# Low weight parts of every second unit: a VectorE subtraction replaced by a ScalarE copy and an accumulating DMA

## The chip, the cores and the metric

The kernel runs on one core of one Trainium2 chip. The time is device microseconds of one launch, from the first to the last instruction of the core and what lies around it; lower is better. The core has TensorE (matrix products, PE in the profile), VectorE (DVE), ScalarE (ACT), GpSimd (POOL) and SyncE (SP), each with a queue of its own that it works through in order, and 16 DMA engines that all queues share.

## What is computed

One block of a streaming encoder over 256 frames of width 2048, in float32. In the reference's words, cut to what matters:

```python
x = x + 0.5 * swiglu(rms_norm(x, ffn1_norm), ffn1_w_gate, ffn1_w_up, ffn1_w_down)
proj = rms_norm(x, mix_norm) @ w_in
x = x + concatenate([pool_mixer(...), gla_mixer(...)]) @ w_out
x = x + mem_cross_attention(rms_norm(x, xattn_norm), rms_norm(mem, mem_norm), w_q, w_kv, w_o)
x = x + 0.5 * swiglu(rms_norm(x, ffn2_norm), ffn2_w_gate, ffn2_w_up, ffn2_w_down)
return rms_norm(x, final_norm)
```

The feed-forward width is 5632, there are 256 memory tokens, 4 heads. What takes the time are the products with the large weights; all weights together are some 400 MB, and each is read once.

## The kernel before

**Two parts for each number.** TensorE's fast float32 form, fp32r, keeps fewer bits of a number than float32. So every operand is written as a sum of two fp32r tiles: the high part (the number rounded by the write) and the low part (number minus high part). A product is the sum of three: high x high, high x low and low x high. Activations are stored as such pairs in `xs` and `ys`, weights are split while they stream in.

**Groups and units.** Weights stream in groups of 512 rows by 512 columns (1 MB), loaded by SP into one of three `raw` buffers (`wload`, L317). A group has two units of 256 rows each (part 0 and part 1). For each unit `split_unit` (L971) makes a high tile `wh` and a low tile `wl` of 128 x 1024: through `split` (L217), ScalarE casts raw to `wh` (L218), and VectorE subtracts, `wl = raw - wh` (L219). There are four buffers of each (`AHEAD` + 1), so the tiles of a unit can only be written when TensorE has done with those of the unit four back.

**Two kinds of block.** In `block_a` (L259) the weights are the stationary operand: a unit is eight pairs of matmuls, one of `wh` with 512 columns (high and low activations side by side), one of `wl` with 256 columns. In `block_b` (L290) the activations are stationary, and a unit is twelve matmuls of 512 columns, one in three with `wl`. A block has mostly four groups (K = 2048) and ends with an eviction from PSUM by ScalarE and VectorE (`joined`, L252, and what follows it; the residual additions at L398).

**What sets the order.** `Stream.emit` (L69) runs through the units in order. Before the matmuls of unit u it emits the splits up to unit u+3, and behind the split of a group's last part the load of the group three further on. The load therefore waits for the last reader of the `raw` buffer that it overwrites. Evictions and norms are put between units by counts. The program is then scheduled as a whole with a timeline model (L1011), which may place instructions of one engine in another order than they are written, where the dependences allow it.

Of the kernel before, what the change touches and what calls it, by code (L numbers as in the profile page):

```python
# [9 lines left out]
AF = mybir.ActivationFunctionType  # L10
ALU = mybir.AluOpType
# [73 lines left out]
def build(ctx, tc, I, out):  # L85
    nc = tc.nc
# [130 lines left out]
    def split(hi, lo, src):  # L217
        nc.scalar.copy(hi, src)  # L218
        nc.vector.tensor_tensor(out=lo, in0=src, in1=f32(hi), op=ALU.subtract)  # L219
# [751 lines left out]
    def split_unit(g, part, last, own):  # L971
        raw = raws.pop(g) if last else raws[g]
        hi, lo = (
            wpool.tile([P, 2, NB], F32R, tag=t, name=f"{t}{g}_{part}", bufs=st.AHEAD + 1)
            for t in ("wh", "wl")
        )
        if own:
            own((hi, lo), raw)
        else:
            step = 1 if g == part == 0 else 2  # L980
            for k in range(0, 2, step):
                src = raw[:, 2 * part + k : 2 * part + k + step, :]
                split(hi[:, k : k + step, :], lo[:, k : k + step, :], src)
        return hi, lo
# [4 lines left out]
    for g in range(st.RAW):  # L989
        load(g)  # L990
    st.emit(load, split_unit)


# [30 lines left out]
```

## Time and profile before

| | us |
|---|---|
| time before, median of 2 runs (2193.71 to 2194.71) | 2194.21 |
| the profiled execution's own time | 2194.78 |
| its span, first to last instruction | 2192.7 |
| TensorE busy | 2173.8 |
| VectorE busy | 1320.3 |
| ScalarE busy | 1037.2 |
| GpSimd busy | 14.3 |

The granted TensorE clock is 0.998 over the span. The profile is of one execution. A line such as `L218 ACT CAST wh<-raw ... x756 | 792.5, 1049 | 1015.2 <-PE pa L280 746.6` is a group of instructions: line 218, on ScalarE, writes a `wh` tile from a `raw` tile, 756 times, 792.5 us busy in sum, 1049 ns each; ahead of them ScalarE sat idle for 1015.2 us, and 746.6 of it ended when TensorE's matmuls of L280 released it. The chain of waits is followed back from the last instruction and says on which engine the time of the end hangs. In the list of DMA issues the last number is the time from issue to landing. In a timeline a row has its start, its length, and in brackets how long its engine idled before and what released it.

### The profile page before, as it was taken

Reading aid. Unit: us, or ns where it says so; the run is one execution under the profiler, and the core shown is the slowest. Engines: PE = TensorE matmul, PEld = TensorE weight load, DVE = VectorE, ACT = ScalarE, POOL = GpSimd, SP = SyncE. Lnnn points to the kernel's source line nnn. Section 1 sums busy time; section 2 is a strip of 40 time slices with the busy share of each in tenths; the row PEclk is TensorE's granted clock in tenths of the full one; section 3 lists DMA queues with packets and bytes.
Section 4 is the critical chain, followed back from the end, with each engine's and each line's share of the span. In section 5 each row is a group of like instructions: output and inputs, shape, how many; then the busy total and the mean of one; then the engine's idle time right before and its main releaser. Section 6 shows DMA issues by size and latency. Waiting matters only on the chain.

```text
span 2192.7 us, 29165 instructions
## 1 busy us (share of the span) xinstructions
PE 2173.8 (99%) x11990; PEld 1876.5 (86%) x11990; DVE 1320.3 (60%) x1518; ACT 1037.2 (47%) x1273; POOL 14.3 (1%) x43
## 2 busy tenths in 40 slices
PE   8999999999999999999999999999999999999997
PEld 7888888888888888888888888888888888888886
DVE  6656556565566777667665555655655565545655
ACT  6444344443444546465455444554443444434443
POOL 0000000000000000000000000000000000000001
PEclk9999999999999999999999999999999999999999
DMA  7555555555555555565555445555555555555553
GB/s 252 185 184 188 192 184 182 191 181 188 189 191 176 191 175 176 157 221 179 189 175 177 168 160 186 191 176 185 182 189 193 191 189 182 187 194 189 192 185 122
DMA packets 205901, 404.79 MB, mean 185 GB/s; under 512 B 8644, under 2 KB 11816, under 8 KB 205384
## 3 DMA queue, kind: packets, MB, share of 16 engines
q1 hardware_dynamic: 205736, 402.92, 55.1%
q8 instruction: 94, 1.54, 0.3%
q14 instruction: 39, 0.32, 0.0%
q10 hardware_dynamic: 32, 0.01, 0.0%
HBM read 400.80 MB, written 2.10 MB: 184 GB/s over the span
## 4 chain that ended last, share of the span: by engine, by line
PE 98%; DMA 1%; DVE 1%; ACT 0%; SPq 0%; issue 0%; DVEq 0%; ACTq 0%
PE pa L280 79%; PE pb L306 14%; PE pe L880 3%; DMA raw<-in_ffn_w_gate 1%; PE pv L816 1%; PE pl L781 1%; DMA rows<-in_x 0%; PE ps L207 0%; PE pa L539 0%; DVE wl L219 0%; PE po L662 0%; PE pb L850 0%; PE tm L740 0%; PE pq L649 0%; DVE Xn L929 0%; PE pn L199 0%
## 5 line engine op out<-in xcount | busy, mean ns | idle before, releaser
L219 DVE TENSOR_TENSOR wl<-raw,wh 128x1024 fp32r<-128x1024 f32 (+1 forms) x755 | 922.1, 1222 | 789.4 <-ACT wh L218 785.2
L280 PE MATMUL pa<-xs,wh 128*128 128x512 f32 x3712 | 1309.6, 398 | 2.1 <-DVE xs L211 2.0
L218 ACT CAST wh<-raw 128x1024 fp32r<-128x1024 f32 (+1 forms) x756 | 792.5, 1049 | 1015.2 <-PE pa L280 746.6
L280 PE MATMUL pa<-xs,wl 128*128 128x256 f32 x3712 | 1031.4, 281 | 0.0
L280 PEld LDWEIGHTS pa<-xs,wh 128*128 128x128 f32 x3712 | 694.2, 188 | 166.0 <-DVE xs L211 3.1
L280 PEld LDWEIGHTS pa<-xs,wl 128*128 128x128 f32 x3712 | 701.5, 189 | 5.9
L280 PE MATMUL pa<-ys,wh 128*128 128x512 f32 x1216 | 428.6, 398 | 0.0
L280 PE MATMUL pa<-ys,wl 128*128 128x256 f32 x1216 | 338.2, 281 | 0.0
L280 PEld LDWEIGHTS pa<-ys,wh 128*128 128x128 f32 x1216 | 227.5, 188 | 54.7
L280 PEld LDWEIGHTS pa<-ys,wl 128*128 128x128 f32 x1216 | 229.7, 189 | 1.8
L306 PE MATMUL pb<-wh,ys 128*128 128x512 f32 x512 | 157.9, 389 | 0.0
L306 PE MATMUL pb<-wh,xs 128*128 128x512 f32 x384 | 122.5, 393 | 0.4 <-DVE ys L211 0.4
L306 PEld LDWEIGHTS pb<-wh,ys 128*128 128x128 f32 x512 | 96.1, 188 | 19.9
L254 ACT COPY c<-pa 128x512 f32<-128x512 f32 x116 | 67.7, 584 | 67.4 <-PE pa L280 67.4
L306 PE MATMUL pb<-wl,ys 128*128 128x512 f32 x256 | 99.6, 389 | 0.0
L306 PEld LDWEIGHTS pb<-wh,xs 128*128 128x128 f32 x384 | 71.9, 188 | 15.3 <-DVE ys L211 0.6
L306 PE MATMUL pb<-wl,xs 128*128 128x512 f32 x192 | 75.0, 390 | 0.0
L880 PE MATMUL pe<-wh,ys 128*128 128x512 f32 x192 | 59.3, 389 | 0.0
L306 PEld LDWEIGHTS pb<-wl,ys 128*128 128x128 f32 x256 | 48.1, 188 | 10.0
L255 DVE TENSOR_TENSOR t<-pa,c 128x512 f32<-128x512 f32 x64 | 44.0, 688 | 18.3 <-ACT c L254 18.3
L398 DVE SCALAR_TENSOR_TENSOR X<-pa,X 128x512 f32<-128x512 f32 x80 | 51.5, 686 | 0.1
L880 PEld LDWEIGHTS pe<-wh,ys 128*128 128x128 f32 x192 | 36.0, 188 | 7.5
(174 smaller groups left out, 810.4 us busy)
## 6 DMA issues: line engine op xcount, KB each, us to landing
raw<-in_ffn_w_up SPq DMA_DIRECT2D x88, 1024.0 KB, 5.0
raw<-in_ffn_w_gate SPq DMA_DIRECT2D x86, 1024.0 KB, 4.9
raw<-in_ffn_w_down SPq DMA_DIRECT2D x84, 1024.0 KB, 4.9
raw<-in_w_in SPq DMA_DIRECT2D x32, 1024.0 KB, 5.3
raw<-in_xattn_w_kv SPq DMA_DIRECT2D x32, 1024.0 KB, 5.2
raw<-in_w_out SPq DMA_DIRECT2D x16, 1024.0 KB, 4.9
raw<-in_xattn_w_q SPq DMA_DIRECT2D x16, 1024.0 KB, 4.9
raw<-in_xattn_w_o SPq DMA_DIRECT2D x16, 1024.0 KB, 4.9
```

Of the source, the lines that this page charges most:

```text
L218: nc.scalar.copy(hi, src)
L219: nc.vector.tensor_tensor(out=lo, in0=src, in1=f32(hi), op=ALU.subtract)
L254: nc.scalar.copy(c, ps[:, :, S:])
L255: nc.vector.tensor_tensor(out=dst, in0=ps[:, :, :S], in1=c, op=ALU.add)
L280: nc.tensor.matmul(o, w, x, start=k == 0 and i == 0, stop=last and i == 1)
L306: nc.tensor.matmul(held["ps"][:, h, :], a, w[:, kk, :], start=k == 0 and i == 0, stop=k == n_k - 1 and i == 2,)
L398: nc.vector.scalar_tensor_tensor(out=xk, in0=part, scalar=scale, in1=xk, op0=ALU.mult, op1=ALU.add)
L781: nc.tensor.matmul(ps[:, t, :M], ys[:, 4 * h + d, a, tok], xa["K"][:, d, b, :], start=i == 0, stop=i == 11,)
L816: nc.tensor.matmul(ps[:, d, :S], xa["V"][:, m, a, col], xa["PT"][:, m, b, :], start=i == 0, stop=i == 5,)
L880: nc.tensor.matmul(acc_ps[nb][:, h, :], a, w[:, kk, :], start=nb in first and kk == 0 and i == 0, stop=k == nk - 2 and kk == 1 and i == 2,)
```

## The change

Only `split_unit` changes. For part 1 of every group from group 8 on, except a group with a split of its own, the low part is made without VectorE. ScalarE casts raw to `wh` as before, then writes `wl` as -1 times raw, which the write rounds to the negative high part; then a DMA that GpSimd issues adds the raw weights to `wl`, from SBUF to SBUF. The sum is again raw minus its high part. Part 0 of every group, the first eight groups, and everything else stay as they are written.

```diff
@@ -976,6 +976,11 @@
         )
         if own:
             own((hi, lo), raw)
+        elif g >= 8 and part == 1:
+            src = raw[:, 2 * part : 2 * part + 2, :]
+            nc.scalar.copy(hi, src)
+            nc.scalar.activation(lo, src, AF.Copy, scale=-1.0)
+            nc.gpsimd.dma_start(out=lo, in_=src, accum_op=ALU.add)
         else:
             step = 1 if g == part == 0 else 2
             for k in range(0, 2, step):
```

## The prediction

> **What bounds the kernel now.** I read the page's busy times first, then the chain that ended last, then its groups.
>
> ```profile
> span 2192.7 us, 29165 instructions
> PE 2173.8 (99%) x11990; PEld 1876.5 (86%) x11990; DVE 1320.3 (60%) x1518; ACT 1037.2 (47%) x1273; POOL 14.3 (1%) x43
> ...
> PE 98%; DMA 1%; DVE 1%; ACT 0%; SPq 0%; issue 0%; DVEq 0%; ACTq 0%
> PE pa L280 79%; PE pb L306 14%; PE pe L880 3%; DMA raw<-in_ffn_w_gate 1%; PE pv L816 1%; PE pl L781 1%; DMA rows<-in_x 0%; PE ps L207 0%; PE pa L539 0%; DVE wl L219 0%; PE po L662 0%; PE pb L850 0%; PE tm L740 0%; PE pq L649 0%; DVE Xn L929 0%; PE pn L199 0%
> ...
> L219 DVE TENSOR_TENSOR wl<-raw,wh 128x1024 fp32r<-128x1024 f32 (+1 forms) x755 | 922.1, 1222 | 789.4 <-ACT wh L218 785.2
> ...
> L218 ACT CAST wh<-raw 128x1024 fp32r<-128x1024 f32 (+1 forms) x756 | 792.5, 1049 | 1015.2 <-PE pa L280 746.6
> ```
>
> TensorE is 98% of the chain; VectorE, the engine that is relieved, is 1% of it, some 22 us of the span. So the edit can gain at most those 22 us, and it loses whatever makes TensorE wait. VectorE's subtraction mostly waits for ScalarE's high part, and ScalarE's high part mostly waits for TensorE to give a buffer back: both engines run after TensorE, with time to spare. How much to spare is the question, and the timeline of one stretch answers it.
>
> ```profile
> 994.50 1.05 ACT L218 CAST wh<-raw 128x1024 fp32r<-128x1024 f32 x1 [0.44 <-PE pa L280]
> 997.39 1.05 ACT L218 CAST wh<-raw 128x1024 fp32r<-128x1024 f32 x1 [1.84 <-PE pa L280]
> ...
> 999.72 0.40 PE L280 MATMUL pa<-ys,wh 128*128 128x512 f32 x1
> 999.96 0.28 PE L280 MATMUL pa<-ys,wl 128*128 128x256 f32 x1
> ...
> 1000.08 0.40 PE L280 MATMUL pa<-ys,wh 128*128 128x512 f32 x1
> ...
> 1000.16 1.05 ACT L218 CAST wh<-raw 128x1024 fp32r<-128x1024 f32 x1 [1.71 <-PE pa L280]
> ...
> 1001.24 1.23 DVE L219 TENSOR_TENSOR wl<-raw,wh 128x1024 fp32r<-128x1024 f32 x1 [0.70 <-ACT wh L218]
> ...
> 1002.98 1.05 ACT L218 CAST wh<-raw 128x1024 fp32r<-128x1024 f32 x1 [1.77 <-PE pa L280]
> ...
> 1005.82 1.05 ACT L218 CAST wh<-raw 128x1024 fp32r<-128x1024 f32 x1 [1.78 <-PE pa L280]
> ```
>
> One pair of matmuls (high, then low) takes 0.36 us (999.72 to 1000.08), a unit of eight pairs 2.83 us; the casts follow each other at 2.82 and 2.84 us. There are four wh and four wl buffers, so a cast starts when TensorE has ended the unit four back, and its own unit begins three units later: 3 x 2.83 = 8.5 us. Cast and subtraction take 1.05 + 1.23 of it. About 6 us are spare at every unit, for both parts.
>
> **The change part by part.** It applies to one unit in two from group 8 on: by the code 369 units.
>
> *VectorE loses* 369 x 1.222 = 451 us of 1320. *ScalarE gains* a second pass over the same tile. The nearest rows are its other activations:
>
> ```profile
> L210 ACT ACTIVATE xs<-X,gains 128x256 fp32r<-128x256 f32 x64 | 28.9, 498 | 3.1 <-DVE X L398 3.0
> L229 ACT ACTIVATE t<-X 128x512 f32<-128x512 f32 x21 | 13.0, 617 | 0.0
> ```
>
> 256 further elements cost 0.12 to 0.21 us (617 - 498; CAST: (1049 - 617)/2), so 128x1024 takes 0.86 to 1.05 us; I take the cast's 1.05. ScalarE becomes 1037 + 387 = 1424 us, 65% of the span, hidden in the 1015 us that it idles before L218. If that cover went, each 0.1 us would come on top of the wait below.
>
> *The accumulating DMA* takes the subtraction's place between ScalarE and TensorE. No such DMA is in the trace, so it is bounded by the plain ones.
>
> ```profile
> q1 hardware_dynamic: 205736, 402.92, 55.1%
> ...
> raw<-in_w_out SPq DMA_DIRECT2D x16, 1024.0 KB, 4.9
> ...
> raw<-in_ffn_w_down SPq DMA_DIRECT2D x8, 512.0 KB, 4.3
> ...
> out<-Xn SPq DMA_DIRECT2D x8, 256.0 KB, 2.2
> ```
>
> A packet of about 2 KB takes 0.551 x 16 x 2192.7 / 205736 = 0.094 us of one DMA engine. A 1 MB load is 512 packets, 32 for each engine, 3.0 us; of its 4.9 us to landing 1.9 are not data. The accumulate writes 512 KB, and to add it must read raw and wl. If that costs as much as a copy: 16 x 0.094 = 1.5 us, with 1.9 landing after 3.4 us. If both reads pass one after the other: 3.0 us, landing after 4.9. The engines are in use by weight loads for 55% of the time; where the two meet and share, I give each half, so 3.0 becomes 3.0 / (1 - 0.55/2) = 4.1 us and the landing 1.9 + 4.1 = 6.0 us. Behind a whole load it would be 1.9 + 3.0 + 3.0 = 7.9 us. Ends: 3.4 and 7.9 us. I take 6.0, nearest to the 1 MB row, because it moves 1 MB in and 0.5 MB out, and because what no row shows (the add itself, GpSimd's issue) can only lengthen it.
>
> [...]
>
> *What is moved: TensorE's order.* The compiled order of the changed kernel is not that of before with one wait changed. In 118 of the 369 units TensorE's low-part matmuls now stand behind work of the next unit: the last half group of a block runs two high matmuls, then the next block's first unit, and only then its other 14. That widens the window of these units and narrows that of the unit which takes over their buffers. I count, unit by unit, the matmuls between the moment at which the negative copy may start (buffer given back, high part done) and the first matmul on the new low part, at 0.24 us for a 512-column and 0.12 for a 256-column matmul. In the commonest narrow place these are 14 leftover matmuls (2.36 us), one unit (2.83) and two high matmuls (0.47), less the high copy's 1.05: 4.6 us. All 369 windows: 42 average 4.6 us, 16 average 5.6, 10 average 6.4, 60 average 7.5, the other 241 are 8 us or more.
>
> The negative copy, the DMA and some 0.25 us of signalling must fit in: 1.05 + 6.0 + 0.25 = 7.3 us. The sum: 42 x (7.3 - 4.6) = 113; 16 x 1.7 = 27; 10 x 0.9 = 9; the rest fits. Together 149 us of TensorE waits, in some 70 places. All matmuls behind the waiting one wait too, and nothing makes it up, since the chain is TensorE.
>
> *Covered moves.* SP's load of group g+3 waited for the subtraction and now waits for the accumulate's landing, 1.05 + 6.0 - 1.2 = 5.8 us later:
>
> ```profile
> ACT wh L218 <- DMA raw<-in_ffn_w_gate: 7.3, 4, 3.6
> ```
>
> ```profile
> SPq L317 <- DVE wl L219: 1817.1, 348, 8.7
> ```
>
> These two rows are from the waits of the compute engines and of the DMA queue (total us, times, longest). ScalarE waited for a load 4 times in all; SP, on the other hand, always waited for its buffer. From a buffer's release to the cast that needs its next load are five units, 14.2 us, of which 0.1 + 1.05 + 1.23 + 4.9 = 7.3 are used; 6.9 spare against 5.8, and the cast itself has 6 us more ahead of TensorE. So it costs nothing; without that cover 1 us of lateness costs up to 1 us per group. GpSimd's queue holds nothing else in these stages than the next accumulates, each long after the last; its seven final-norm products come when the last accumulate is done. SP's queue keeps its order.
>
> The profiled execution took 2194.78 us, 2.1 more than its span and 0.6 above the median of 2194.21. Predicted: 2194.8 + 149 = 2344 us.
>
> **The rivals.**
>
> *The accumulate is hidden (not slower).* Place: the 42 windows of 4.6 us. If it lands 3.4 us after issue, as a copy would, 1.05 + 3.4 + 0.25 = 4.7 us and the loss is 42 x 0.1 = 4 us: 2198 us. For this speaks the 256 KB row's 2.2 us; against it the 512 KB row's 4.3. It decides at 4.3 us: then 42 x 1.0 + a little = 44 us, 2%. A gain beyond 2% would need 44 us from VectorE's 22, which I give 1 in 100.
>
> *The DMA engines become the bound.* Loads use 3.0 us of each engine per group; a group lasts two units, 5.66 us. With two reads the accumulate brings it to 6.0, which alone would be 369 x 0.34 = 125 us, still inside the forecast. If the adding costs twice that again (6.0 us), each of 369 groups takes 9.0 us, and the time is 2195 + 369 x 3.3 = 3400; at 4.5 us for the accumulate, 7.5 per group, 2870. For it speaks that one load fills the engines while it lasts:
>
> ```profile
> 1002.00:1004.25 2.25, 2.25 (x15) 1.92 (x14) 0.65 (x2) 1.05 (x1) 0.00 (x0) 1.00 0.98 333
> ```
>
> In this stretch of 2.25 us a load holds 98% of the engines at 333 GB/s, so an accumulate that falls there must push it aside. Against it: the engines idle for the other 45%, and three raw buffers let loads and accumulates take turns.
>
> *ScalarE becomes late.* Where blocks end, evictions queue between its casts, and a second pass of 1.05 us adds to each. With about 94 blocks (376 groups, most blocks of four) and one pass late at each, 94 x 1.05 = 99 us on top of the forecast: 2440. Against it: 1015 us idle before L218.
>
> **How the numbers follow.** Forecast (landing after 4.3 to 7.9 us) 0.62; hidden 0.22, of it 0.01 a gain over 2%; DMA engines as the bound 0.13; ScalarE late 0.03. About 2% is what a measurement of this kernel can tell from no change. So slower 0.62 + 0.13 + 0.03 = 0.78, same 0.21, faster 0.01. At 7.9 us the need is 9.2, and the classes give 42 x 4.6 + 16 x 3.6 + 10 x 2.8 + 60 x 1.7 + 143 x 1.1 (of the 241, those near 8.1) = 538 us, less what one stall gives to the next window in the same block, about a tenth: 484, so 2680, the high end. The low end is 2200, in the hidden case. Outside lie most of the DMA-bound case and the lowest part of the hidden one.
>
> **What would show it.** After: VectorE near 870 us and ScalarE near 1420; 369 new DMAs landing about 6 us after issue; TensorE's idle time before low-part matmuls of changed units near 150 us, on fewer than 100 places, put down to the DMA; DMA share near 0.8 to 0.95. Wrong would be: no TensorE idle time (hidden); waits at nearly every changed unit with the DMA share at its ceiling (the DMA engines); waits of TensorE put down to the high part (ScalarE).

## The result and the profile after

The changed kernel takes 2474.85 us (median of 2 runs, 2465.56 and 2484.13) against 2194.21: a ratio of 1.128, with a 95% interval of 1.110 to 1.146. Forecast were 2344 in a range of 2200 to 2680. The profiled execution is the longer one, 2484.13 us.

The page of the changed kernel first: busy times, DMA share by slices, DMA queues, and the chain that ended last.

```profile
span 2482.3 us, 30449 instructions
PE 2264.5 (91%) x11990; PEld 1920.2 (77%) x11990; DVE 885.2 (36%) x1149; ACT 1376.5 (55%) x1642; POOL 332.3 (13%) x412
...
DMA  7988999899898888899898999889899888898997
...
q1 hardware_dynamic: 205736, 402.92, 47.9%
q0 software_dynamic: 53136, 193.49, 41.1%
...
DMA 42%; PE 33%; issue 19%; ACT 5%; POOL 1%; DVE 1%; SPq 0%; POOLq 0%; ACTq 0%; DVEq 0%
DMA wl<-raw 37%; PE pa L280 23%; PE pb L306 7%; ACT wl L982 3%; DMA raw<-in_ffn_w_down 2%; PE pe L880 1%; POOL wl L983 1%; DMA raw<-in_ffn_w_up 1%; DMA raw<-in_w_out 1%; DMA raw<-in_w_in 1%; DMA raw<-in_ffn_w_gate 0%; ACT wh L981 0%; DMA rows<-in_x 0%; DMA raw<-in_xattn_w_o 0%; ACT wh L218 0%
```

VectorE and ScalarE moved by what the change takes and gives, and neither matters. The chain, which was TensorE to 98%, is now a transfer to 42%, and 37 of the 42 are the new one, `wl<-raw`. The span grew by 289.6 us. TensorE's busy time explains 90.7 of them (2264.5 - 2173.8), its idle time the other 198.9. The same page's groups (busy and mean ns, then idle before them with what ended it) and its DMA issues (KB each, median us from issue to landing) say where that idle time stands:

```profile
L280 PE MATMUL pa<-xs,wh 128*128 128x512 f32 x3712 | 1330.7, 405 | 0.5 <-DVE xs L211 0.5
L280 PE MATMUL pa<-xs,wl 128*128 128x256 f32 x3712 | 1025.2, 288 | 120.7 <-DMA wl<-raw 120.3
...
L982 ACT ACTIVATE wl<-raw 128x1024 fp32r<-128x1024 f32 x369 | 390.0, 1057 | 103.3 <-PE pb L306 74.9
...
L280 PE MATMUL pa<-ys,wl 128*128 128x256 f32 x1216 | 335.5, 289 | 50.8 <-DMA wl<-raw 50.3
...
L306 PE MATMUL pb<-wl,ys 128*128 128x512 f32 x256 | 103.3, 403 | 18.2 <-DMA wl<-raw 18.2
...
wl<-raw POOLq DMA_DIRECT2D x369, 512.0 KB, 6.1
raw<-in_ffn_w_up SPq DMA_DIRECT2D x88, 1024.0 KB, 5.7
```

TensorE stands still before low parts (`wl`) and hardly ever before high parts (0.5 us), and what it stands for is the landing of the accumulate. Matched one by one with the matmuls of the written kernel, there are 102 such waits of over half a microsecond, all on low parts that the change makes. Measured from the start of one matmul to the start of the next, less the 0.24 us that a matmul takes, they come to 214 us. The waits of the engines (total us, times, longest) name them again and show who else is held up:

```profile
PEld pa L280 <- DMA wl<-raw: 211.6, 104, 5.2
POOL wl L983 <- DMA wl<-raw: 209.5, 41, 7.6
...
ACT wh L218 <- DMA raw<-in_ffn_w_down: 73.9, 33, 4.7
ACT wh L218 <- DMA raw<-in_ffn_w_gate: 69.9, 39, 4.0
...
ACT wh L218 <- DMA raw<-in_ffn_w_up: 52.5, 29, 3.8
```

ScalarE's casts waited for loads 4 times in 7.3 us before; now these three rows alone have 101 waits and 196 us. The POOL row is no such wait, though it names one accumulate as waiting for another: in the trace all 41 of these issues start 0.29 to 0.31 us after ScalarE has written the negative copy, as nearly all the others do.

Most of the other 91 us, TensorE being busy for longer, comes from its clock. The mean granted clock is 0.968, against 0.998 before; 0.032 x 2482.3 - 0.002 x 2192.7 = 75 us. The rest is the difference between the two ways of measuring the waits (214 against 199 us). The timeline of TensorE at one wait, and the table of stretches behind it (length, then busy us of PE, PEld, DVE, ACT, POOL; granted clock; DMA share; GB/s), show how the one follows from the other:

```profile
223.81 0.62 PE L280 MATMUL pa<-ys,wh 128*128 128x512 f32 x2
228.34 0.39 PE L280 MATMUL pa<-ys,wl 128*128 128x256 f32 x1 [3.92 <-DMA wl<-raw]
```

```profile
225.00:229.00 4.00, 0.66 (x4) 0.62 (x5) 0.00 (x0) 0.43 (x1) 0.00 (x0) 0.99 1.03 221
229.00:232.41 3.41, 3.41 (x13) 2.94 (x12) 1.83 (x2) 1.19 (x3) 0.00 (x0) 0.51 0.90 299
232.41:236.00 3.59, 3.59 (x22) 3.12 (x21) 0.00 (x0) 2.73 (x3) 0.86 (x1) 1.00 0.83 317
```

After 3.92 us without work TensorE runs for 3.41 us at half its clock: 13 matmuls where the next 3.59 us hold 22. So such a wait is paid twice, once in full, and once in half of the window behind it. Not every wait is: behind the 102 waits there are 38 stretches at half clock.

### The profile page after: what moved, and what is told of

It is laid out like the page before. It is cut to its first block, busy times and chain, and to the rows that moved or that the text cites. A ratio compares the mean times of both kernels' runs of the same rounds, so it can differ in the third digit from the quotient of the medians.

```text
span 2482.3 us, 30449 instructions
## 1 busy us (share of the span) xinstructions
PE 2264.5 (91%) x11990; PEld 1920.2 (77%) x11990; DVE 885.2 (36%) x1149; ACT 1376.5 (55%) x1642; POOL 332.3 (13%) x412
## 3 DMA queue, kind: packets, MB, share of 16 engines
q1 hardware_dynamic: 205736, 402.92, 47.9%
q0 software_dynamic: 53136, 193.49, 41.1%
## 4 chain that ended last, share of the span: by engine, by line
DMA 42%; PE 33%; issue 19%; ACT 5%; POOL 1%; DVE 1%; SPq 0%; POOLq 0%; ACTq 0%; DVEq 0%
DMA wl<-raw 37%; PE pa L280 23%; PE pb L306 7%; ACT wl L982 3%; DMA raw<-in_ffn_w_down 2%; PE pe L880 1%; POOL wl L983 1%; DMA raw<-in_ffn_w_up 1%; DMA raw<-in_w_out 1%; DMA raw<-in_w_in 1%; DMA raw<-in_ffn_w_gate 0%; ACT wh L981 0%; DMA rows<-in_x 0%; DMA raw<-in_xattn_w_o 0%; ACT wh L218 0%
## 5 line engine op out<-in xcount | busy, mean ns | idle before, releaser
L280 PE MATMUL pa<-xs,wh 128*128 128x512 f32 x3712 | 1330.7, 405 | 0.5 <-DVE xs L211 0.5
L219 DVE TENSOR_TENSOR wl<-raw,wh 128x1024 fp32r<-128x1024 f32 (+1 forms) x386 | 471.6, 1222 | 1253.8 <-ACT wh L218 1247.0
L280 PEld LDWEIGHTS pa<-xs,wl 128*128 128x128 f32 x3712 | 722.2, 195 | 168.6 <-DMA wl<-raw 149.1
L280 PEld LDWEIGHTS pa<-xs,wh 128*128 128x128 f32 x3712 | 703.2, 193 | 148.0 <-DVE xs L211 1.6
L218 ACT CAST wh<-raw 128x1024 fp32r<-128x1024 f32 (+1 forms) x387 | 405.2, 1047 | 449.1 <-PE pa L280 121.6
L981 ACT CAST wh<-raw 128x1024 fp32r<-128x1024 f32 x369 | 386.5, 1047 | 434.4 <-PE pa L280 433.9
L983 POOL DMA_DIRECT2D wl<-raw x369 | 318.5, 863 | 2129.9 <-ACT wl L982 1845.7
L982 ACT ACTIVATE wl<-raw 128x1024 fp32r<-128x1024 f32 x369 | 390.0, 1057 | 103.3 <-PE pb L306 74.9
L280 PEld LDWEIGHTS pa<-ys,wl 128*128 128x128 f32 x1216 | 236.6, 195 | 70.0 <-DMA wl<-raw 62.5
```

What stands on the lines that cost most here:

```text
L280: nc.tensor.matmul(o, w, x, start=k == 0 and i == 0, stop=last and i == 1)
L982: nc.scalar.activation(lo, src, AF.Copy, scale=-1.0)
L983: nc.gpsimd.dma_start(out=lo, in_=src, accum_op=ALU.add)
```

## The experiments

The theory after the result: TensorE waits for the landing, which comes late because the accumulate holds each DMA engine for 2.76 us (41.1% of 2482.3 us over 369) and meets the loads; a drop of the granted clock (0.968 over the span) follows. The rivals: the forecast's own step, that the new order of TensorE's matmuls makes the narrow windows; ScalarE's second pass; DMA engines that are simply full; a shortage of buffers in only one of the two loops (the tiles `wh` and `wl`, or `raw`); the size of one transfer. Times are of one execution beside one of the kernel before on the same chip, unless more are named; the kernels are called e1 to e11.

### Without the accumulate, and with a copy in its place

```diff
-            nc.gpsimd.dma_start(out=lo, in_=src, accum_op=ALU.add)
```

> Left out: the accumulating DMA, so the low parts of the changed units hold only the negative high part. ScalarE's second pass and VectorE's relief stay. If the DMA is the whole cause (my theory): 2190 to 2205 us, no TensorE wait on a low part. If ScalarE's second pass of 1.05 us is a part of it: 2250 us or more, with TensorE waits put down to ScalarE's L982.

e1: 2192.3 us, before 2195.38. ScalarE's second pass and VectorE's relief are there, and they cost nothing. TensorE's new order is not: with the DMA left out the program was scheduled anew, and at 11909 of 11990 places its matmuls work on the same tiles as in the kernel before, against 9444 in the changed kernel. So e1 does not test the order; e2 and e3 do. Its busy times:

```profile
PE 2174.2 (99%) x11990; PEld 1877.2 (86%) x11990; DVE 891.3 (41%) x1149; ACT 1375.4 (63%) x1642; POOL 14.3 (1%) x43
```

The next kernel puts a plain copy in the accumulate's place:

```diff
-            nc.gpsimd.dma_start(out=lo, in_=src, accum_op=ALU.add)
+            nc.gpsimd.dma_start(out=lo, in_=src)
```

> The same GpSimd-issued DMA without the add: it copies raw over the low part (left out: the subtraction, low part = raw). If the price lies in reading both operands: time on the DMA engines falls from 2.76 us to about 1.4 us of each engine, the median landing from 6.1 to about 4.5 us, DMA share from 0.89 to near 0.75, time 2210 to 2280 us. If it lies in GpSimd's issue and the fixed part of a DMA: landing stays at 5.5 us or more and the time above 2380 us.

e2: 2239.73 us, before 2195.38: a DMA that only copies still costs 44 us. Its matmuls stand in the changed kernel's order at all 11990 places. Its rows on the page, the queues and the landing:

```profile
q1 hardware_dynamic: 205736, 402.92, 54.9%
q0 software_dynamic: 53136, 193.49, 24.5%
...
wl<-raw POOLq DMA_DIRECT2D x369, 512.0 KB, 4.8
```

A copy holds each of the 16 engines for 0.245 x 2238.0 / 369 = 1.49 us, the accumulate (41.1% of 2482.3) for 2.76 us: 1.9 times as long, for the same bytes written. Row by row (4 KB) the median is 174 against 328 ns. The order of the matmuls being the same, the step from 2240 to 2475 us is the add, and the first 44 us are what a plain copy of this size costs at this place. The earliest landings are 2.8 us after issue for the copy and 4.4 for the accumulate: 1.3 of the 1.6 us between them are the engines' longer work, and 0.3 are GpSimd, which takes 0.86 us to issue an accumulate and 0.53 to issue a copy. That the longer work is a second read fits the factor of 1.9, but no run shows it apart from the add.

### The order of TensorE's matmuls

```diff
-                            nc.tensor.matmul(
+                            tc.keep_in_program_order(nc.tensor.matmul(
```

(in `block_a` and `block_b`, so that their matmuls keep the order in which they are written)

> The changed kernel with TensorE's weight matmuls kept in the written order, so that no low part is put off and no window is narrower than in the kernel before (all but a few 7.4 us or more, where 68 were under 7). If the narrow windows are the cause: the waits there (102 us) go, the time falls to about 2330 us. If it is the spread of the landing beyond 6 us, with half of all windows near 7.8: the waits only move to other units and the time stays at 2420 us or more. If the DMA engines are the bound: no change, 2470.

e3: 2490.32 us, before 2195.38. Written in order, nearly all windows are 7.4 us or wider by the forecast's own count, and the waits are all still there. In the waits of this kernel:

```profile
PEld pa L280 <- DMA wl<-raw: 197.7, 110, 5.4
...
PEld pb L306 <- DMA wl<-raw: 35.0, 20, 3.2
...
PE ps L207 <- DVE diag L206: 17.7, 7, 3.8
```

The narrow windows are gone and the loss is not, so the rival from the forecast falls. (The last row is the price of the fixed order itself, at the norms: where the order is free, it is not over 2.3 us.)

### More buffers

The next three kernels keep that order. Room for buffers comes from smaller helpers (the identity cut to 128 columns, one buffer fewer for three scratch tiles).

```diff
-    AHEAD = 3
+    AHEAD = 4
```

> As the one before, and with five wh and five wl buffers in place of four (room for it from smaller helper tiles), so that every window is one unit, 2.8 us, longer: about 10.6 us against a need of 1.05 + 0.3 + landing. If latency against the window is the cause: nearly all waits go, 2195 to 2230 us, clock back to 0.99 or more. If the DMA engines (89% busy) are the bound: 2350 us or more, with the landing later instead (8 us or more).

e4: 2368.8 us, before 2195.38. With five `wh` and `wl` each, waits on the landing fall by about half and new ones appear. The waits of this kernel:

```profile
ACT wh L218 <- DMA raw<-in_ffn_w_down: 212.7, 76, 8.7
ACT wh L218 <- DMA raw<-in_ffn_w_up: 185.1, 73, 6.0
ACT wh L218 <- DMA raw<-in_ffn_w_gate: 169.6, 66, 7.0
PEld pa L280 <- DMA wl<-raw: 101.9, 82, 3.7
```

Now it is ScalarE that waits, for the `raw` loads: 567 us in these three rows, 196 in the changed kernel. The expectation that nearly all of the loss goes with longer windows was wrong; the median landing, 6.9 us, is later than the changed kernel's, but not the 8 us or more of the other expectation.

```diff
-    RAW = 3
+    RAW = 4
```

> TensorE's matmuls in written order, four wh and wl buffers as in the changed kernel, but four raw buffers in place of three (same smaller helper tiles as the five-buffer run). If the loads that wait for an accumulate's landing before they may overwrite raw are what leaves the DMA engines idle: the waits of ScalarE on raw go, DMA share 0.94 or more, time 2300 to 2400 us. If the windows of wl alone count: no change, 2470 to 2490 us.

e5: 2479.25 us, before 2194.75. Four `raw` buffers alone change nothing: ScalarE's waits for loads are gone but for 3 us, and TensorE's 123 waits on the landing (177 us of idle time) are left:

```profile
PE pa L280 <- DMA wl<-raw: 150.2, 103, 4.3
PE pb L306 <- DMA wl<-raw: 22.1, 14, 3.2
...
PE pe L880 <- DMA wl<-raw: 4.9, 6, 1.4
```

Both together:

```diff
-    AHEAD = 3
-    RAW = 3
+    AHEAD = 4
+    RAW = 4
```

(and the attention's output moved into buffers that are free by then)

> TensorE's matmuls in written order with both pools deeper at once: five wh and wl buffers and four raw buffers (room from smaller helper tiles and from the tile of the attention output, which moves into buffers that are free by then). Each alone left 2369 and 2479 us. The side accumulates showed that the DMA engines can carry all 369 accumulates in 2203 us when nobody waits for one of them. If the loss is the landing (7.4 us there) against a budget of 6.4 us for wl, and the load that comes after it against three raw buffers: with both budgets longer 2200 to 2240 us, DMA share 0.97 or more, clock 0.99. If something else holds: above 2300.

e9: 2260.35 us, before 2194.27. Of 281 us, 215 are gone, which is between the two expectations. The busy times and the queues of its page, and two rows of TensorE's waits:

```profile
PE 2200.5 (97%) x11990; PEld 1892.3 (84%) x11990; DVE 883.6 (39%) x1149; ACT 1379.2 (61%) x1642; POOL 332.3 (15%) x412
...
q1 hardware_dynamic: 205736, 402.92, 52.2%
q0 software_dynamic: 53136, 193.49, 45.5%
...
wl<-raw POOLq DMA_DIRECT2D x369, 512.0 KB, 7.6
```

```profile
PE ps L207 <- DVE diag L206: 21.3, 7, 4.4
PE pa L280 <- DMA wl<-raw: 17.8, 13, 3.7
```

The accumulates land later than in the changed kernel, 7.6 us after issue against 6.1, and TensorE hardly waits. So the landing is late against the window, not late by itself. Of the 66 us that are left, 21 stand in the row of the fixed order, 18 in waits on the landing, and 0.011 x 2258.6 - 4 = some 20 in the clock (0.989); the few that remain were not placed.

### DMA engines that are full

The kernel before (with the smaller helpers), and beside it as many accumulates of the same size into two scratch tiles that nobody reads (allocated and set to zero in lines not shown):

```diff
+            if g >= 8 and part == 1:
+                nc.gpsimd.dma_start(out=side[g % 2], in_=f32(hi), accum_op=ALU.add)
```

> The kernel before, unchanged in its result, and beside it the same 369 accumulating DMAs of 512 KB, from the high part onto a tile that nobody reads: nothing on TensorE waits for them and raw is not held by them (with the smaller helper tiles). If the DMA engines are full: their work of some 2210 to 2260 us per engine is over TensorE's 2190, loads land late (7 us or more), ScalarE waits for raw, 2230 to 2330 us. If only the wait for the landing counts: 2195 to 2205 us.

e7: 2202.83 us, before 2194.75. From its page:

```profile
PE 2177.6 (99%) x11990; PEld 1879.4 (85%) x11990; DVE 1318.3 (60%) x1518; ACT 1036.7 (47%) x1273; POOL 333.6 (15%) x414
...
q0 software_dynamic: 53136, 193.49, 51.6%
q1 hardware_dynamic: 205736, 402.92, 48.9%
...
side<-wh POOLq DMA_DIRECT2D x369, 512.0 KB, 7.4
...
raw<-in_ffn_w_down SPq DMA_DIRECT2D x84, 1024.0 KB, 9.0
```

The two queues hold all 16 engines all the time, loads take 9.0 us where they took 4.9, and the kernel loses 8 us. Full engines are not the loss; at TensorE's full pace they make the accumulate land after 7.4 us, and that is a loss where TensorE waits for it.

### Fewer, and smaller, accumulates

```diff
-        elif g >= 8 and part == 1:
+        elif g >= 8 and part == 1 and g % 2 == 0:
```

> The change for every second group only, so one unit in four: 184 or 185 accumulates. If the DMA engines are the bound (load 3.1 and accumulate 2.76 us of each engine per group, 5.86 against TensorE's 5.66): work per group falls to 4.5 us, landing falls to about 5 us, and nearly the whole loss goes: 2195 to 2235 us. If the latency of each accumulate against its window counts alone: half of the loss stays, 2320 us or more.

e6: 2191.47 us, before 2194.75: with the change at one unit in four (184 accumulates) nothing is lost. The same kernel with more runs:

> The change for every second group again, timed in five rounds against the kernel before, since one look gave 2191.5 against 2194.8 us. If VectorE's relief is worth the few us that its waits hold on the chain: 2190 to 2193 us, ratio 0.998 to 0.999. If the one look was scatter: ratio 1.000 within its interval.

e11: 2190.92 us (median of 11 runs) against 2194.84 (median of 15 runs, 14 of them from 2193.98 to 2196.82 and one of 4356.07): ratio 0.9985, interval 0.9976 to 0.9994. With the whole work of the kernel done, it is the one version ahead of both kernels, by 0.15%, far less than the 2% from which a change counts. Its landing, beside TensorE's busy time:

```profile
PE 2165.7 (99%) x11990; PEld 1871.9 (86%) x11990; DVE 1103.4 (50%) x1334; ACT 1209.1 (55%) x1457; POOL 173.6 (8%) x227
...
wl<-raw POOLq DMA_DIRECT2D x184, 512.0 KB, 4.7
```

```diff
-        elif g >= 8 and part == 1:
+        elif g >= 8 and part == 1 and g % 3 < 2:
```

> The change for two groups of three (every group 2193 to 2484 us, every second group 2191). Work of each DMA engine per group: 3.1 + 2/3 x 2.76 = 4.9 us of TensorE's 5.66, 87%. If the loss comes from accumulates that share the engines with loads, it starts here: landing about 5.3 us, 2210 to 2300 us, and less than two thirds of the loss of the full change (187 us). If each accumulate costs the same by itself: 2380.

e10: 2306.01 us, before 2194.27, with 246 accumulates, in two groups out of three and none in the third. The median landing is 5.7 us, and TensorE has 63 waits on it, 78 us of idle time together. Two thirds of the accumulates cost 40% of the loss (112 of 281), one half none of it. The largest row of these waits:

```profile
PE pa L280 <- DMA wl<-raw: 62.8, 53, 3.2
```

The last kernel splits each accumulate in two:

```diff
-            nc.gpsimd.dma_start(out=lo, in_=src, accum_op=ALU.add)
+            for k in range(2):
+                nc.gpsimd.dma_start(out=lo[:, k, :], in_=src[:, k, :], accum_op=ALU.add)
```

> The accumulate as two DMAs of 256 KB each (one per 128 rows), so that TensorE may start on the first half while the second is still under way; engine work is the same. If latency counts: the first half lands 1.4 us earlier and the time falls by 50 to 120 us. If the DMA engines are the bound: within 30 us of 2475; slower if GpSimd's issue (0.86 us each) adds up.

e8: 2507.45 us, before 2194.75, slower than the changed kernel where a gain of 50 to 120 us had been expected of a shorter landing:

```profile
wl<-raw POOLq DMA_DIRECT2D x738, 256.0 KB, 6.0
```

Two transfers of half the size land 6.0 us after issue each in the median, no sooner than one whole, and GpSimd issues the second one 0.9 us after the first. Halving the transfer does not help.

## Why the prediction was right, and where it was not

*The sign and the mechanism hold.* TensorE bounds the kernel, VectorE's relief brings nothing (e1 is 3 us ahead of before), and TensorE waits for the accumulate's landing. ScalarE's second pass is hidden, as forecast: 1375 us (forecast 1424) with no loss in e1; one pass took 1.057 us (forecast 1.05).

*The price of the accumulate holds.* An accumulate takes 2.76 us of each engine (forecast 3.0, as two reads one after the other); its median landing is 6.1 us (6.0), and the engines were busy for 0.89 of the span (0.8 to 0.95). That the median came so close is in part luck, since the landings spread from 4.4 to 10.2 us. Whoever would take a copy's price is off by the 235 us between e2 and the changed kernel, and even a copy lands 4.8 us after issue in the median, not 3.4, so the rival "hidden" had its end too low.

*The step that failed is "TensorE's order".* The forecast put 149 us on 68 units with windows under 7 us that the order makes. In the trace those units have 39 of the 102 waits and 102 us; the other 63 waits, 112 us, stand at units with wider windows that were to lose nothing. And the narrow ones were not needed: e3 has almost none and is as slow. What the forecast missed is the spread. It set one landing of 6.0 us against each window; sorted, the 369 landings are 5.2 us at the lower quarter, 6.1 in the middle, 7.8 at the upper quarter and 9.3 at the 95th of 100. An ordinary window of 8 us less the second pass (1.05) and signals (0.3; the forecast's 0.25 stood in no row, and 0.29 to 0.31 us lie between ScalarE's write and GpSimd's issue) leaves 6.6, which 149 of the 369 overrun. That the result lies inside the range of 2200 to 2680 is therefore in part luck: its high end is one landing of 7.9 us for all units, and the clock is not in it.

*Why the landings spread* follows from sums that the forecast had in hand for a rival: the accumulate's 2.76 us and a load's 3.1 (0.479 x 2482.3 / 384; the queue's 402.92 MB are 384 loads' worth) make 5.9 us of engine time per group, and a group lasts 5.66 at TensorE's pace. The forecast priced that overrun as 0.34 us a group, "inside the forecast". e7 measures it as throughput: 8 us in all. Its real effect is on latency: in e7, with TensorE at 99% and both queues together at 100% of the engines, the landing is 7.4 us. With half as many accumulates (e11) it is 4.7. The changed kernel's trace shows the sharing one by one: 163 of its 369 accumulates met loads that took under 0.5 us of each engine between 1.0 and 4.4 us after their issue, and landed after 5.1 us in the median; the 132 that met 2 us or more landed after 8.3. So the spread is mostly whether a load is under way, which the forecast had averaged to 55%.

*The "covered move" was not free, but it is not what decides either.* The loads that wait for the accumulate come late (196 us of ScalarE's waits). Alone this costs nothing, since e5 takes these waits away and gains nothing; but with the first loop widened it is the next bound (e4), and only both together let the kernel run (e9).

*One term was missing.* The clock: some 75 us of the 290, behind the waits. The forecast 149 us and the 290 by which the span of the profiled execution grew thus differ by 65 us of waits (214 less 149) and 75 us of clock.

*What stays open:* why one unit in four is 0.15% ahead. Less work on VectorE and another order of the matmuls are two guesses that no run tells apart. e1, with no accumulate at all and nearly the order of before, is as far ahead, but that is one run. Two more things are open: why the add holds the engines longer than the copy, and what the kernel would take with the loads moved so that no accumulate meets one.

## What to carry to other kernels

A transfer put between two engines is to be compared, at the load that the DMA engines will then have, with the window that the buffers leave, and not its median (6.1 us here) but its late end (9.3 at the 95th of 100). The add held each engine for 2.76 us here, a copy of the same size for 1.49. With the engines busy for 0.89 of the span, each of the two loops that end in a transfer needed one buffer more here (e9); the other way out is to make the change at fewer units (half of the accumulates cost nothing in e11, two thirds 112 us in e10). And where TensorE is the bound, a wait can cost more than its own length: half clock followed 100 of the 180 waits of 2 to 3 us counted below.

## What the runs showed of the hardware

**TensorE's granted clock halved after some waits of over 1 us.** All 170 windows at half clock (0.51 granted in the one shown above) in the twelve traces of the changed kernel and the experiments (the first 60 and last 30 us left out) follow an idle stretch of TensorE. The table has these stretches by their length, from the start of one matmul to the start of the next less 0.24 us:

| TensorE idle, us | stretches | followed by half clock |
|---|---|---|
| 0.5 to 1 | 161 | 0 |
| 1 to 2 | 249 | 8 |
| 2 to 3 | 180 | 100 |
| 3 to 4 | 55 | 44 |
| over 4 | 18 | 18 |

A window lasts 3.41 us (146 of them) or twice that (24). In the seven traces with more than five such windows, all of them start on one grid of 3.413 us per trace; in the changed kernel's, the 38 starts lie within 0.002 us of it. Of the 36 idles of 2 to 3 us in that trace, half clock follows 17; each of the other 19 is split between two windows of the grid, with at most 2.00 us in one. The second table counts the windows of the seven traces that are not at half clock themselves, with all idle stretches of 0.1 us and more.

| TensorE idle in one window of 3.41 us, in sum | windows | followed by half clock |
|---|---|---|
| under 1 | 4064 | 0 |
| 1 to 2 | 349 | 22 |
| 2 to 2.25 | 53 | 45 |
| over 2.25 | 99 | 99 |

**Full DMA engines by themselves cost 8 us here.** With both queues at 100% together (e7) a load took nearly twice as long to land (9.0 against 4.9 us), TensorE stayed at 99%, and the kernel lost 8 us of 2195.
